# A two-layer encoder with eight experts: 20 weight slots of 1 MB in place of 17, and two branches a scatter in place of four

## The chip, the cores and the metric

The kernel runs on one core of a Trainium2 chip. Time is device time in microseconds from the start to the end of one execution. The core has five engines with a queue of instructions each: PE (matrix products into PSUM), DVE (vector), ACT (scalar functions), POOL and SP. SP issues the weight DMAs. Engines wait for each other by semaphores.

## The reference

Two layers over 272 tokens (16 meta tokens and 256 of input) of width 1024. Each layer has four mixers and a feed-forward part; that of the second layer is a mixture of eight experts, of which each token takes two:

```python
logits = (t @ router).astype(jnp.float32)
top_v, top_i = lax.top_k(logits, TOP_K)
gates = jax.nn.softmax(top_v, axis=-1)
combine = jnp.sum(jax.nn.one_hot(top_i, N_EXPERTS) * gates[..., None], axis=1)
out = jnp.zeros_like(t)
for e in range(N_EXPERTS):
    out = out + combine[:, e:e + 1] * _swiglu(t, wg[e], wu[e], wd[e])
```

with `_swiglu(u, wg, wu, wd) = (silu(u @ wg) * (u @ wu)) @ wd`. An expert is 3584 wide, all in float32, and the eight of them have 352 MB of weights. After the second layer comes a last RMSNorm.

## The kernel before

**Up to the experts.** Layer 1, then the mixers of layer 2 and its output projection. While that projection runs, `stat_logit` (L1262) turns the residual back to rows of tokens (`hr`) and takes the sums of squares (L1281, with a scratch tile `jk` that nobody reads). Then the router picks two experts for each token and counts the tokens of each expert.

**An expert.** Its tokens are gathered by a product with a 0/1 matrix (`pick`, tile `xe`, up to 96 tokens). The 3584 columns go in 7 steps of 512. A step has four weight tiles of 1 MB for the gate and up products (`gate_up`, tiles `gu` and `gx`) and two for the down product (`down`, tile `dn`, summed in PSUM over the steps). 8 experts of 7 steps of 6 tiles are 336 DMAs. Each product has a first part for 64 tokens and a second part for the other 32 that is executed only if the expert has more than `CA` = 64 tokens: `more` (L1380) puts it under `tc.If(n > CA)`, a conditional branch on PE. In the text an expert with more is heavy, one with fewer is light.

**The order on PE** is the program's own order (a manual schedule, L1547): in step i the first half of `gate_up`, then `between`, then the second half, then the down product of step i-1. `between` turns the activations of step i-1 (`turn_sg`, PSUM tile `ehT`, copied out by ACT at L1468 into `eh`). In the third step of an expert it also scatters the expert before.

**The scatter** (L1506) adds the gated result `oe`, and `oe4` for tokens 65 to 96, to the tokens' rows. The result has two halves `i` of 512 columns and two halves `j` of 128 tokens, so four products into four PSUM tiles `sct`. Each has a first matmul (L117), two conditional ones (a pair, L116), and an addition to `acc` on DVE (L1517). `ehT`, `sct` and the tiles of `turn` and `pick` share two PSUM banks in turn: `pp = lambda n='pp': bank('pp', n, 2)`. The scatter of expert 7 follows at the end of the program, and after it the last norm (`final`), which reads the weight row `fin` and writes squares to `jk`.

**The weight tiles.** `eload` gives each tile the next slot in a fixed rotation that a string names by pool: b (4 slots), c (6), a (3), o (2), and u and U, two tiles of the dense part that have become free; 17 in all. One further slot (h) serves once, and becomes `acc`. SP issues the DMAs in the order of use and waits before each until its slot has been read. `ahead` issues the first 18 as soon as their memory is free, during the output projection.

Of the kernel before, what the change touches and what calls it, by code (L numbers as in the profile page):

```python
# [9 lines left out]
F32 = mybir.dt.float32  # L10
# [4 lines left out]
ALU = mybir.AluOpType  # L15
# [6 lines left out]
D = 1024  # L22
DC = 8
# [4 lines left out]
C = 96  # L28
# [80 lines left out]
def build(tc, A, out, off):  # L109
    nc = tc.nc  # L110
    ctx = ExitStack()
    V, SC, GP, PE = nc.vector, nc.scalar, nc.gpsimd, nc.tensor

    def mm(o, a, b, start=True, stop=True, skip=False):
        if skip:
            return PE.matmul(o, a, b, start=start, stop=stop, skip_group_check=True)  # L116
        return PE.matmul(o, a, b, start=start, stop=stop)  # L117
# [3 lines left out]
    def bank(tag, name, bufs):  # L121
        return ps.tile([128, 512], F32, tag=tag, name=name, bufs=bufs)

    pp = lambda n='pp': bank('pp', n, 2)
# [113 lines left out]
    bs = mb_('stat')  # L238
# [18 lines left out]
    for a0, w in ((0, 272), (272, 271)):  # L257
        b = mb_('fb')
# [908 lines left out]
    with tc.tile_pool(name='fw', bufs=1, reuse_waits='tile') as fw, \  # L1167
# [22 lines left out]
        def fload(*a):  # L1190
            fcnt[0] += 1
            return wload({'a': wa, 'b': wb}['aaabb'[(fcnt[0] - 1) % 5]], *a)
# [3 lines left out]
        def fsplit(w):  # L1196
            scnt[0] += 1
            k, f = w.shape[1], w.shape[2]
            if scnt[0] % 3 != 2:
                hl = [fw.tile([128, 2048], F32R, tag='fw', name='fw', bufs=4)[:, :k * f].rearrange('p (k f) -> p k f', k=k)  # L1200
                      for _ in range(2)]
                split(*hl, w)
                return [[t[:, i] for i in range(k)] for t in hl]
            k = k // 2
            hl = [], []
            for i in range(2):
                t = wo.tile([128, 2048], F32R, tag='w', name='wx')
                t = [t[:, 1024 * p_:1024 * p_ + k * f].rearrange('p (k f) -> p k f', k=k) for p_ in range(2)]
                split(*t, w[:, k * i:k * i + k])
                for p_ in range(2):  # L1210
                    hl[p_].extend(t[p_][:, kk] for kk in range(k))
            return hl
# [25 lines left out]
        for m2 in range(4):  # L1238
            b = [(mb_, bm, pp)[m2 % 3]('dn') for _ in range(2)]
            for k0, nk in ((0, 8), (8, 8), (16, 6)):  # L1240
                w = fsplit(fload(A['ffn_w_down'][0, 128 * k0:128 * (k0 + nk), 256 * m2:256 * m2 + 256], nk, 256))
# [4 lines left out]
            for mi in range(2):  # L1246
                m = 2 * m2 + mi
                t = fp.tile([128, L], F32, name='sg', tag='sg', bufs=2)
# [14 lines left out]
    def stat_logit(h, m):  # L1263

        if not lgp:
            lgp.append(bm('lg'))
        with tc.manual_schedule(engines={mybir.EngineType.PE}):
            for j in range(2):
                t0 = TOK[j][0]
                mm(lgp[0][:, NE * j:NE * j + NE], h[:, t0:t0 + 128], rt[:, m, :], start=(m == 0 and j == 0),  # L1270
                   stop=(m == DC - 1), skip=True)
        n, c = m // 4, m % 4
        if c == 0:
            hrb.extend(bm('hr') for _ in range(2))
        for j in range(2):
            t0 = TOK[j][0]
            PE.transpose(hrb[j][:, 128 * c:128 * c + 128], h[:, t0:t0 + 128], ident)
        if c == 3:
            for j in range(2):
                jk = ep.tile([128, 512], F32, name='jk', tag='jk', bufs=2)  # L1280
                SC.activation(jk, hrb[j], AF.Square, accum_out=sj[:, 2 * j + n:2 * j + n + 1])  # L1281
            for j in range(2):
                SC.copy(hr[:, j, 512 * n:512 * n + 512], hrb[j])
            del hrb[:]
# [3 lines left out]
    wb = ctx.enter_context(tc.tile_pool(name='wb2', bufs=4, side='right', reuse_waits='tile'))  # L1288
    mq = ctx.enter_context(tc.tile_pool(name='mq', bufs=1, reuse_waits='tile'))
    ep = ctx.enter_context(tc.tile_pool(name='ep', bufs=1, reuse_waits='tile'))  # L1290
# [4 lines left out]
    def rstd_rows(r, ss):  # L1295
        V.tensor_scalar(r, ss, 1.0 / D, EPS, op0=ALU.mult, op1=ALU.add)
        GP.tensor_tensor(r, r, nhalf[:, :2], op=ALU.pow)
# [38 lines left out]


    cnt, wdma = [0], []
    wc = ctx.enter_context(tc.tile_pool(name='wc', bufs=6, reuse_waits='tile'))
    slots = {'a': wa, 'b': wb, 'c': wc, 'o': wo}  # L1340
    wm = A['moe_w']
    nb = FE // 512
# [21 lines left out]
    def dn_units(w, fb):  # L1364
        return [(w[fb, u], 2) for u in (4, 5)]

    first, order = 'bbbbccccccaaaoouUh', 'bbbbccccccaaaoouU'

    def ahead(slots_, i):

# [10 lines left out]
    def more(n, body):  # L1381

        if n is None:
            return body()
        with tc.If(n > CA):  # L1385
            body()
# [41 lines left out]
    def new_xe():  # L1428
        return ep.tile([128, DC, C], F32, name='xe', tag='xe', bufs=2)
# [32 lines left out]
    def turn_sg(sg, s4):  # L1462
        b = pp('ehT')
        for i in range(2):
            PE.transpose(b[:, 128 * i:128 * i + 128], sg[:, 128 * i:128 * i + 128], ident)  # L1465
        PE.transpose(b[:, 256:384], s4, ident)  # L1466
        eh = ep.tile([128, 384], F32, name='eh', tag='eh', bufs=2)
        SC.copy(eh, b[:, :384])  # L1468
        return eh
# [35 lines left out]

    def scatter(oe, oe4, GT, GT4, n, to, fro):  # L1506
        for i in range(2):
            for j in range(2):
                b = pp('sct')
                mm(b, GT[:, 128 * j:128 * j + 128], oe[:, i])  # L1510

                def rest():
                    for p_ in range(2):
                        mm(b, GT4[:, 128 * j:128 * j + 128], oe4[p_][:, i], start=False, stop=(p_ == 1), skip=True)

                more(n, rest)
                V.tensor_tensor(to[:, j, 512 * i:512 * i + 512], fro[:, j, 512 * i:512 * i + 512], b, op=ALU.add)  # L1517

    sel_of = lambda e: select([rk[:, j, e:e + 1] for j in range(2)], [gat[:, j, e:e + 1] for j in range(2)], rx)
    banks = lambda: [bm('dn') for _ in range(3)]  # L1520
# [49 lines left out]
                sgs[i] = act(*bgu)  # L1570


    def final(fin, res):
        for n in range(2):
            fs = slice(512 * n, 512 * n + 512)
            for j in range(2):
                h = acc[:, j, fs]
                jk = ep.tile([128, 512], F32, name='jk', tag='jk', bufs=2)
                SC.activation(jk, h, AF.Square, accum_out=sj[:, 2 * j + n:2 * j + n + 1])  # L1579
                (GP if j in [1] else V).tensor_tensor(res[:, j, fs], h, fin[:, fs], op=ALU.mult)  # L1580
        V.tensor_tensor(rj, sj[:, 0::2], sj[:, 1::2], op=ALU.add)  # L1581
        rstd_rows(rj, rj)
        for j in range(2):
            for n in range(2):
                fs = slice(512 * n, 512 * n + 512)
                if (j, n) == (0, 1):
                    SC.activation(res[:, j, fs], res[:, j, fs], AF.Copy, scale=rj[:, j:j + 1])
                else:
                    V.tensor_scalar(res[:, j, fs], res[:, j, fs], rj[:, j:j + 1], None, op0=ALU.mult)  # L1589
            nc.sync.dma_start(out[0, 128 * j:128 * j + 128, :], res[:, j])  # L1590

    with tc.high_priority(200):
        eh = turn_sg(*sgs.pop(i))
    fin = ep.tile([128, D], F32, name='fin', tag='fin')
    finish(i, eh)
    with tc.issue_after(wdma[-1].ins):
        SP.dma_start(fin, A['final_norm_w'][None, :].to_broadcast([128, D]))
    scatter(*gated(dn[NE - 1], T_[NE - 1][2]), *T_[NE - 1][:2], nr[NE - 1], acc, acc)
    res = up.tile([128, DC * L], F32, name='res', tag='uTl')[:, :2 * D].rearrange('p (j f) -> p j f', j=2)
    final(fin, res)  # L1600


    most = nc.values_load(mxi[0:1, 0:1], min_val=0, max_val=S)  # L1603
    with tc.If(most > C):
        rk2 = ep.tile([128, 2, NE], F32, name='rk2')
        V.tensor_copy(rk2, rk)
        order = 'abab'
        for _ in range((S - 1) // C):
            V.tensor_scalar(rk2, rk2, -float(C), None, op0=ALU.add)
            with tc.For_i(0, NE, 1) as e:  # L1610
                rc = ep.tile([128, 2, 2], F32, name='rc')
                V.tensor_copy(rc[:, 0, :], rk2[:, :, bass.ds(e, 1)].rearrange('p j o -> p (j o)'))
                V.tensor_copy(rc[:, 1, :], gat[:, :, bass.ds(e, 1)].rearrange('p j o -> p (j o)'))
                w = wm[bass.ds(e, 1)].rearrange('o b u p f -> (o b) u p f')
                sl = select([rc[:, 0, j:j + 1] for j in range(2)], [rc[:, 1, j:j + 1] for j in range(2)], rx)
                GT, GT4, gc = turn(*sl)
                xe = new_xe()
                for k4 in range(2):
                    pick(xe, sl[2], k4)
                do = banks()  # L1620
                for fb in range(nb):
                    down(do, turn_sg(*act(*gate_up(xe, w, fb, None))), w, fb, None)
                scatter(*gated(do, gc), GT, GT4, None, acc, acc)
        fin = ep.tile([128, D], F32, name='fin', tag='fin')
        GP.dma_start(fin, A['final_norm_w'][None, :].to_broadcast([128, D]))
        final(fin, res)
    ctx.close()


# [43 lines left out]
```

## Time and profile before

| | |
|---|---|
| median of 3 runs | 1489.84 us (1486.25 to 1493.8) |
| the profiled execution | 1490.97 us |
| its span, first to last instruction | 1489.1 us |
| PE busy | 1424.5 us, 96% |
| DVE, ACT, POOL busy | 537.5, 356.0, 81.0 us |
| granted clock of PE, mean | 0.978 |
| moved by DMA | 429.22 MB, mean 288 GB/s |

A row of the table of stretches has, in this order, the busy time of PE, of PE's weight loads, of DVE, ACT and POOL. Two views are read below by their idle time: a row of the timeline has the start, the time taken and, in brackets, how long the engine had been idle and who ended that. A row of the waits adds such idle time up by who ended it. A busy engine isn't necessarily one at its full speed, and a wait for several semaphores is put down to the one that came last.

### The profile page before, as it was taken

The page shows a single profiled execution, that of the slowest core. Times are in us where ns is not written, and L with a number is a line of the kernel's source. Part 1 is how long each engine was busy: PE and PEld are TensorE (multiplying, and loading weights), DVE is VectorE, ACT ScalarE, POOL GpSimd, SP SyncE. Part 2 cuts the span into 40 slices and gives each one's busy share as a digit, 9 for nine tenths or more (in the row PEclk, how much of TensorE's full clock was granted, in tenths as well). Part 3 has the DMA queues.
Part 4 walks back from the last instruction along what each step waited for, and adds up shares of the span by engine and source line. Part 5 has one row for each costly group of instructions (what it writes and reads, how often), then busy time and mean ns, then how long its engine had stood idle before and what let it go on. Part 6 is the DMA issues. An engine that isn't in the chain of part 4 may idle for free. (4 is left out here: it accounts for less than half of the span.)

```text
span 1489.1 us, 30433 instructions
## 1 busy us (share of the span) xinstructions
PE 1424.5 (96%) x13288; PEld 1011.9 (68%) x13288; DVE 537.5 (36%) x1179; ACT 356.0 (24%) x716; POOL 81.0 (5%) x77
## 2 busy tenths in 40 slices
PE   7999989999989999999999999999999999999996
PEld 6887789999988869656555565455555455555552
DVE  6885476555667775200211200211200211202102
ACT  4544344444453543000100100100100101101002
POOL 4141000000012300000000000000000000000000
PEclk9999699999999999999999999999999999999998
DMA  9521075555433309888999999999999999999980
GB/s 278 164 86 57 1 218 171 180 167 165 126 100 116 112 31 414 317 341 339 384 418 417 418 419 376 390 418 419 418 412 373 405 418 419 417 417 420 419 338 31
DMA packets 116442, 429.22 MB, mean 288 GB/s; under 512 B 7900, under 2 KB 69852, under 8 KB 73008
## 3 DMA queue, kind: packets, MB, share of 16 engines
q1 hardware_dynamic: 116032, 425.48, 73.6%
q8 instruction: 140, 2.29, 0.6%
q0 software_dynamic: 240, 1.19, 0.2%
q14 instruction: 30, 0.25, 0.0%
HBM read 425.59 MB, written 2.17 MB: 287 GB/s over the span
## 5 line engine op out<-in xcount | busy, mean ns | idle before, releaser
L116 PE MATMUL gu<-w,xe 128*64 128x256 f32 x3584 | 411.7, 382 | 12.6 <-PEq L1385 7.9
L116 PEld LDWEIGHTS gu<-w,xe 128*64 128x64 f32 x3584 | 261.3, 137 | 168.4 <-issue 64.5
L116 PE MATMUL dn<-w,eh 128*64 128x512 f32 (+1 forms) x1344 | 257.1, 598 | 8.1 <-PEq L1385 7.7
L116 PEld LDWEIGHTS dn<-w,eh 128*64 128x64 f32 (+1 forms) x1344 | 77.1, 127 | 156.3 <-issue 155.2
L1459 DVE TENSOR_TENSOR es<-es,gx 128x128 f32<-128x128 f32 x56 | 16.1, 287 | 422.5 <-ACT es L1458 422.5
L1468 ACT COPY eh<-ehT 128x384 f32<-128x384 f32 x56 | 26.8, 478 | 466.1 <-PE ehT L1466 457.8
L116 PE MATMUL gx<-w,xe 128*32 128x128 f32 x3584 | 109.4, 274 | 0.0
L116 PEld LDWEIGHTS gx<-w,xe 128*32 128x32 f32 x3584 | 94.4, 110 | 21.5 <-issue 21.5
L142 ACT CAST wx<-w 128x1024 fp32r<-128x1024 f32 (+2 forms) x86 | 87.9, 1026 | 68.2 <-PE wo L1132 16.7
L143 DVE TENSOR_TENSOR wx<-w,wx 128x1024 fp32r<-128x1024 f32 (+2 forms) x75 | 89.7, 1202 | 33.7 <-ACT wx L142 33.4
L1458 ACT ACTIVATE es<-gx 128x128 f32<-128x128 f32 x56 | 15.5, 277 | 288.4 <-PE gx L116 171.0
L1132 PE MATMUL wo<-mixh,wx 128*128 128x272 f32 (+1 forms) x256 | 58.8, 311 | 6.0 <-DVE hT L1135 4.9
L1424 DVE TENSOR_TENSOR xe<-xe,fwc 128x384 f32<-128x384 f32 x16 | 8.9, 558 | 144.6 <-PE xe L117 144.6
L143 DVE TENSOR_TENSOR fw<-w,fw 128x2048 fp32r<-128x2048 f32 (+1 forms) x23 | 50.6, 2199 | 26.4 <-ACT fw L142 26.4
L1132 PEld LDWEIGHTS wo<-mixh,wx 128*128 128x128 f32 x256 | 44.2, 197 | 12.8 <-DVE hT L1135 6.3
L142 ACT CAST fw<-w 128x2048 fp32r<-128x2048 f32 (+1 forms) x23 | 42.1, 1832 | 37.0 <-PE dn L160 16.2
L1580 POOL TENSOR_TENSOR res<-acc,fin 128x512 f32<-128x512 f32 x2 | 2.9, 1458 | 881.4 <-DVE acc L1517 881.4
L1517 DVE TENSOR_TENSOR acc<-acc,sct 128x512 f32<-128x512 f32 x28 | 18.9, 687 | 51.5 <-PEq L1385 35.1
L161 PE MATMUL g<-uTh,fw 128*128 128x272 f32 x128 | 37.0, 289 | 0.0
L160 PE MATMUL g<-uTl,fw 128*128 128x272 f32 x128 | 36.8, 288 | 0.0
L159 PE MATMUL g<-uTh,fw 128*128 128x272 f32 x128 | 36.5, 288 | 0.0
L1134 PE MATMUL wo<-mixl,wx 128*128 128x272 f32 (+1 forms) x128 | 35.0, 295 | 0.0
(488 smaller groups left out, 2311.4 us busy)
## 6 DMA issues: line engine op xcount, KB each, us to landing
w<-in_moe_w SPq DMA_DIRECT2D x336, 1024.0 KB, 14.7
w<-in_w_in SPq DMA_DIRECT2D x20, 1024.0 KB, 5.3
w<-in_ffn_w_gate SPq DMA_DIRECT2D x11, 1024.0 KB, 5.5
w<-in_ffn_w_up SPq DMA_DIRECT2D x11, 1024.0 KB, 5.4
w<-in_w_out SPq DMA_DIRECT2D x8, 1024.0 KB, 5.0
w<-in_ffn_w_down SPq DMA_DIRECT2D x8, 1024.0 KB, 5.3
w<-in_ffn_w_down SPq DMA_DIRECT2D x4, 768.0 KB, 4.5
w<-in_w_in SPq DMA_DIRECT2D x4, 512.0 KB, 5.7
```

Of the source, the lines that this page charges most:

```text
L116: return PE.matmul(o, a, b, start=start, stop=stop, skip_group_check=True)
L142: a = SC.copy(hi, src)
L143: return a, (eng or V).tensor_tensor(lo, src, hi.bitcast(F32), op=ALU.subtract)
L159: PE.matmul(o, a[0], b[0], start=start, stop=False)
L160: PE.matmul(o, a[0], b[1], start=False, stop=False)
L161: PE.matmul(o, a[1], b[0], start=False, stop=stop)
L1132: PE.matmul(o, a, mixT[0][:, c0 + k, q0:], start=(p_ == k == 0), stop=(p_ == k == 1))
L1134: PE.matmul(o, a, mixT[1][:, c0 + k, q0:], start=False, stop=False)
L1458: SC.activation(t, b_[:, :w], AF.Silu)
L1459: V.tensor_tensor(t, t, b_[:, w:2 * w], op=ALU.mult)
L1468: SC.copy(eh, b[:, :384])
L1517: V.tensor_tensor(to[:, j, 512 * i:512 * i + 512], fro[:, j, 512 * i:512 * i + 512], b, op=ALU.add)
```

## The change

Pool `wc` gets 9 slots in place of 6, and the rotation 20 in place of 17. Room for them is made in three places: the scratch `jk` of the sums of squares lies in the slots of `xe`, the final norm's row and its scratch in a weight slot of pool b (`last_tiles`), and the memory for POOL's DMA descriptors is set to 8192 bytes. The scatter takes both `j` of a half together: two first matmuls, one branch over both pairs, two additions.

```diff
@@ stat_logit
-                jk = ep.tile([128, 512], F32, name='jk', tag='jk', bufs=2)
+                jk = ep.tile([128, DC, C], F32, name='jk', tag='xe', bufs=2).rearrange('p k c -> p (k c)')[:, :512]
@@
-    wc = ctx.enter_context(tc.tile_pool(name='wc', bufs=6, reuse_waits='tile'))
+    wc = ctx.enter_context(tc.tile_pool(name='wc', bufs=9, reuse_waits='tile'))
@@
-    first, order = 'bbbbccccccaaaoouUh', 'bbbbccccccaaaoouU'
+    first, order = 'bbbbcccccccccaaaoouUh', 'bbbbcccccccccaaaoouU'
@@ scatter
         for i in range(2):
+            bs = [pp('sct') for _ in range(2)]
             for j in range(2):
-                b = pp('sct')
-                mm(b, GT[:, 128 * j:128 * j + 128], oe[:, i])
-
-                def rest():
+                mm(bs[j], GT[:, 128 * j:128 * j + 128], oe[:, i])
+
+            def rest():
+                for j in range(2):
                     for p_ in range(2):
-                        mm(b, GT4[:, 128 * j:128 * j + 128], oe4[p_][:, i], start=False, stop=(p_ == 1), skip=True)
-
-                more(n, rest)
-                V.tensor_tensor(to[:, j, 512 * i:512 * i + 512], fro[:, j, 512 * i:512 * i + 512], b, op=ALU.add)
+                        mm(bs[j], GT4[:, 128 * j:128 * j + 128], oe4[p_][:, i], start=False, stop=(p_ == 1), skip=True)
+
+            more(n, rest)
+            for j in range(2):
+                V.tensor_tensor(to[:, j, 512 * i:512 * i + 512], fro[:, j, 512 * i:512 * i + 512], bs[j], op=ALU.add)
@@
+    def last_tiles():
+        t = wb.tile([128, 2048], F32, name='fin', tag='w')
+        return t[:, :D], [t[:, D + 512 * j:D + 512 * j + 512] for j in range(2)]
...
-    fin = ep.tile([128, D], F32, name='fin', tag='fin')
     finish(i, eh)
     with tc.issue_after(wdma[-1].ins):
+        fin, jks = last_tiles()
         SP.dma_start(fin, A['final_norm_w'][None, :].to_broadcast([128, D]))
...
-    nc = bacc.Bacc("TRN2", target_bir_lowering=False, num_devices=1)
+    nc = bacc.Bacc("TRN2", target_bir_lowering=False, num_devices=1, dynamic_dma_scratch_size=8192)
```

The order on PE, in the first scatter (expert 0, in the third step of expert 1), from its first matmul. The number in `sct_7801` is that of the PSUM tile, and in brackets stands whose semaphore the instruction waits for. Before:

```order
L117 MATMUL sct_7801<-oe_7576,GT_6499 128x512
L1385 COMPARE_AND_BRANCH
L116 MATMUL sct_7801<-oe4_7577,GT_6499 128x512 x2
L1385 UNCONDITIONAL_BRANCH
L1385 UNCONDITIONAL_BRANCH [waits PE_49]
L117 MATMUL sct_7807<-oe_7576,GT_6499 128x512 [waits Activation_49]
L1385 COMPARE_AND_BRANCH
L116 MATMUL sct_7807<-oe4_7577,GT_6499 128x512 x2
L1385 UNCONDITIONAL_BRANCH
L1385 UNCONDITIONAL_BRANCH [waits PE_49]
L117 MATMUL sct_7813<-oe_7576,GT_6499 128x512 [waits DVE_49]
L1385 COMPARE_AND_BRANCH
```

And in the changed kernel:

```order
L117 MATMUL sct_7801<-oe_7576,GT_6505 128x512
L117 MATMUL sct_7802<-oe_7576,GT_6505 128x512 [waits Activation_49]
L1385 COMPARE_AND_BRANCH
L116 MATMUL sct_7801<-oe4_7577,GT_6505 128x512 x2
L116 MATMUL sct_7802<-oe4_7577,GT_6505 128x512 x2
L1385 UNCONDITIONAL_BRANCH
L1385 UNCONDITIONAL_BRANCH [waits PE_49]
L117 MATMUL sct_7812<-oe_7576,GT_6505 128x512 [waits DVE_49]
L117 MATMUL sct_7813<-oe_7576,GT_6505 128x512 [waits DVE_49]
L1385 COMPARE_AND_BRANCH
```

The second first matmul has moved ahead of the branch and of the first pair, with its wait for ACT. Both first matmuls of the second half wait for DVE, as before, but now one behind the other with no branch between them.

The order on DVE in the same scatter (`hr` is the residual, `acc` the sum). Before:

```order
L1517 TENSOR_TENSOR acc_6378<-hr_5939,sct_7801 128x512 [waits DMAHW6_49,PE_49]
L1385 UNCONDITIONAL_BRANCH x2
L1517 TENSOR_TENSOR acc_6378<-hr_5939,sct_7807 128x512 [waits PE_49]
L1517 TENSOR_TENSOR acc_6378<-hr_5939,sct_7813 128x512 [waits PE_49]
L1385 UNCONDITIONAL_BRANCH
L1517 TENSOR_TENSOR acc_6378<-hr_5939,sct_7819 128x512 [waits PE_49]
```

And in the changed kernel:

```order
L1519 TENSOR_TENSOR acc_6384<-hr_5939,sct_7801 128x512 [waits DMAHW1_49,PE_49]
L1519 TENSOR_TENSOR acc_6384<-hr_5939,sct_7802 128x512 [waits PE_49]
L1385 UNCONDITIONAL_BRANCH
L1519 TENSOR_TENSOR acc_6384<-hr_5939,sct_7812 128x512 [waits PE_49]
L1519 TENSOR_TENSOR acc_6384<-hr_5939,sct_7813 128x512 [waits PE_49]
```

The additions stand in pairs between the ends of the branches, each with its own wait for PE.

The order on SP, from the last DMA of the output projection's weights. Before:

```order
L138 DMA w<-in_w_out 128x2x1024 x4
L1352 DMA w<-in_moe_w 128x2048 x18
L1603 TENSOR_LOAD mxi
L1603 ISA x2
L1385 UNCONDITIONAL_BRANCH
L1352 DMA w<-in_moe_w 128x2048 x2
L1385 UNCONDITIONAL_BRANCH
```

And in the changed kernel:

```order
L138 DMA w<-in_w_out 128x2x1024 x4
L1352 DMA w<-in_moe_w 128x2048 x21
L1609 TENSOR_LOAD mxi
L1609 ISA x2
L1385 UNCONDITIONAL_BRANCH
L1352 DMA w<-in_moe_w 128x2048 x2
L1385 UNCONDITIONAL_BRANCH
```

Three more weight DMAs stand ahead of the first one that is tied to the experts' own progress.

## Rows read from the trace of the kernel before

**Rows 1.** Stretches: us, busy time (instructions) by engine, granted clock, DMA share, GB/s.

```profile
602.00:735.00 133.00, 131.81 (x1708) 77.46 (x1708) 17.00 (x48) 9.10 (x26) 0.00 (x0) 1.00 0.88 337
735.00:835.00 100.00, 94.56 (x802) 56.33 (x802) 19.66 (x45) 11.01 (x28) 0.00 (x0) 1.00 1.01 418
```

**Rows 2.** Waits of PE, 600 to 1471 us: total us, times, longest us.

```profile
PE gu L116 <- DMA w<-in_moe_w: 3.3, 4, 1.0
```

**Rows 3.** Timeline of PE near 1345 us: start us, us, instruction, [idle before].

```profile
1344.91 1.30 PE L116 MATMUL gu<-w,xe 128*64 128x256 f32 x10 [0.99 <-PEq L1385]
```

**Rows 4.** Line 1352, 1319.5 to 1320.5 us: one weight DMA.

```profile
L1352 SPq DMA_DIRECT2D w<-in_moe_w x1: 328/328/328, 1319.8 to 1319.8; - x1
...
DMA to landing us min/median/max: 19.9/19.9/19.9
```

**Rows 5.** Line 1352, 557 to 594 us: the first 18 weight DMAs.

```profile
L1352 SPq DMA_DIRECT2D w<-in_moe_w x18: 327/365/448, 557.1 to 593.1; - x18
...
DMA to landing us min/median/max: 4.7/9.9/15.8
```

**Rows 6.** Timeline: a down product of expert 7, issue and first reader of fin.

```profile
1425.60 5.51 PE L116 MATMUL dn<-w,eh 128*64 128x512 f32 x32
...
1430.86 0.33 SPq L1597 DMA_DIRECT2D fin<-in_final_norm_w  x1
...
1475.13 1.27 POOL L1580 TENSOR_TENSOR res<-acc,fin 128x512 f32<-128x512 f32 x1 [879.48 <-DVE acc L1517]
```

**Rows 7.** DMA issues of the whole run: KB each, median us from issue to landing.

```profile
fin<-in_final_norm_w SPq DMA_DIRECT2D x1, 512.0 KB, 20.1
```

**Rows 8.** Timeline: the scatter of expert 0, a heavy one.

```profile
750.50 0.48 PE L117 MATMUL sct<-oe,GT 128*128 128x512 f32 x1
...
750.84 0.48 ACT L1468 COPY eh<-ehT 128x384 f32<-128x384 f32 x1 [8.01 <-PE ehT L1466]
...
751.37 0.50 PE L117 MATMUL sct<-oe,GT 128*128 128x512 f32 x1
...
751.71 0.63 PE L116 MATMUL sct<-oe,GT 128*128 128x512 f32 x2
...
752.38 0.69 DVE L1517 TENSOR_TENSOR acc<-hr,sct 128x512 f32<-128x512 f32 x1 [0.20 <-PE sct L116]
...
753.45 0.62 PE L116 MATMUL sct<-oe,GT 128*128 128x512 f32 x2
...
754.00 2.37 PE L116 MATMUL gu<-w,xe 128*64 128x256 f32 x19
```

**Rows 9.** Timeline: the scatter of expert 1, a light one.

```profile
853.61 0.47 PE L117 MATMUL sct<-oe,GT 128*128 128x512 f32 x1
...
854.48 1.12 PE L117 MATMUL sct<-oe,GT 128*128 128x512 f32 x2 [0.39 <-ACT eh L1468]
...
855.11 2.06 DVE L1517 TENSOR_TENSOR acc<-acc,sct 128x512 f32<-128x512 f32 x3 [0.21 <-PEq L1385]
...
855.85 0.50 PE L117 MATMUL sct<-oe,GT 128*128 128x512 f32 x1 [0.25 <-DVE acc L1517]
...
856.50 2.34 PE L116 MATMUL gu<-w,xe 128*64 128x256 f32 x19
```

**Rows 10.** Instructions on the tile sct, whole run: count, ns min/median/max, first and last.

```profile
L116 PE MATMUL sct<-oe,GT x32: 387/392/398, 750.8 to 1477.2; 128*128 128x512 f32 x32
```

**Rows 11.** Timeline: the scatter of expert 7, at the end.

```profile
1472.67 0.50 PE L117 MATMUL sct<-oe,GT 128*128 128x512 f32 x1 [1.56 <-DVE oe L1500]
...
1473.67 1.38 DVE L1517 TENSOR_TENSOR acc<-acc,sct 128x512 f32<-128x512 f32 x2 [1.05 <-PE sct L116]
...
1475.08 0.76 DVE L1500 SCALAR_TENSOR_TENSOR oe<-dn,gc,oe 64x512 fp32r<-64x512 f32 x1
...
1475.90 0.50 PE L117 MATMUL sct<-oe,GT 128*128 128x512 f32 x1 [1.57 <-DVE oe L1500]
...
1476.99 1.29 DVE L1517 TENSOR_TENSOR acc<-acc,sct 128x512 f32<-128x512 f32 x2
```

More of the change, by code (lines that the diff above doesn't have):

```diff
@@ L1570, in build, with final @@
                 sgs[i] = act(*bgu)
-    def final(fin, res):
+    def last_tiles():
+        t = wb.tile([128, 2048], F32, name='fin', tag='w')
+        return t[:, :D], [t[:, D + 512 * j:D + 512 * j + 512] for j in range(2)]
+    def final(fin, jks, res):
         for n in range(2):
@@ L1577, in final @@
                 h = acc[:, j, fs]
-                jk = ep.tile([128, 512], F32, name='jk', tag='jk', bufs=2)
+                jk = jks[j]
                 SC.activation(jk, h, AF.Square, accum_out=sj[:, 2 * j + n:2 * j + n + 1])
@@ L1599, in build @@
     res = up.tile([128, DC * L], F32, name='res', tag='uTl')[:, :2 * D].rearrange('p (j f) -> p j f', j=2)
-    final(fin, res)
+    final(fin, jks, res)
     most = nc.values_load(mxi[0:1, 0:1], min_val=0, max_val=S)
@@ L1623, in build @@
                 scatter(*gated(do, gc), GT, GT4, None, acc, acc)
-        fin = ep.tile([128, D], F32, name='fin', tag='fin')
+        fin, jks = last_tiles()
         GP.dma_start(fin, A['final_norm_w'][None, :].to_broadcast([128, D]))
-        final(fin, res)
+        final(fin, jks, res)
     ctx.close()
```

## The prediction

> **What bounds the kernel now.** I read the table of stretches first, to see which stage the change lies in. The experts run from 602 to 1471 us of the 1489.1 us span, and TensorE (PE) is busy in nearly all of it: 131.81 of 133 us in the stretch 602 to 735, where the expert has over 64 tokens ("heavy", the conditional part of each product is executed), and 94.56 of 100 us in 735 to 835, where it is skipped ("light") [rows 1]. In the light stretches the DMA engines are full as well (share 1.01, 418 GB/s), so two things could set the pace. A full DMA with a PE that is 95% busy is what a weight-bound loop can look like, so busy shares don't decide it. The second view does: PE's waits between 600 and 1471 us. The wait put down to a weight DMA is 3.3 us in 4 places, at most 1.0 us each [rows 2]. The last of the four places is at 1344.91 us, the first gate product of expert 7, 0.99 us idle, which another view puts down to PE's own sequencer [rows 3]. The weights which that product reads were issued at 1319.8 us and landed 19.9 us later [rows 4], that is at 1339.7, 5.2 us before use. So the four waits are the start of an expert, where the sequencer reads the token count, and no lack of weights. I followed all 336 weight DMAs from landing to first use in the same way, and the stretch around 1340 us is the tightest. **PE alone sets the pace from 602 to 1471 us, and every time added to or taken from PE there goes into the end time in full.**
>
> **The slots.** Three more slots (wc from 6 to 9) let the queue run 3 MB further ahead. At 418 GB/s a slot of 1.05 MB takes 2.5 us, so the lead grows by 3 x 2.5 = 7.5 us wherever the queue had been stopped by full slots. PE takes the same weights at the same time as before, so I cost this at 0. At the start nothing comes late either: the first 18 DMAs are issued by 593.1 us and land within 15.8 us [rows 5], so by 608.9; the three added ones stand behind them and land by about 616, when PE is in its first steps with the tiles that came first.
>
> The places found for the slots cost nothing by the same kind of cover. The scratch of the row sums now lies in the two xe slots: the last write of it precedes the first xe of expert 0 on the way to it. The final norm's row (fin) goes into a weight slot. It was issued at 1430.86 us and is first read at 1475.13; the slot that it takes was last read by a down product that ended at 1431.1 us (1425.60 + 5.51), some 6 us later in the new kernel, and with the 20.1 us that it took to land it is there by 1458 [rows 6, 7]. If that cover failed, it would be POOL and VectorE (DVE) at the end that wait. Halving the descriptor space touches only the four DMAs that POOL issues in the setup of the program.
>
> **The scatter, heavy.** A scatter has two halves; each has two first matmuls, two conditional pairs, two adds on DVE, and two PSUM banks in all. Before, bank 1's pair covered the wait for bank 2, and bank 2's matmuls covered the add of bank 1. Now both banks are taken at once, and the next half can't begin before the first add has ended. Before [rows 8]: first matmul 750.50, second 751.37 (it waits for ACT's copy out of the bank, 750.84 + 0.48), next gate product 754.00: 3.50 us. Now, from the first matmul as 0: the second at 0.87, since it takes the same bank. The pairs follow 0.34 after it (751.37 to 751.71), 0.46 apart (a pair takes 0.63 and a matmul 0.39 [rows 10], so there are about 0.23 between two starts): 1.21 and 1.67; the first is done at 1.84. Its add starts 0.04 later (751.71 + 0.63 to 752.38), 1.88, and takes 0.69: 2.57. The next half's first matmul comes 0.05 after (as 855.11 + 0.69 to 855.85 [rows 9]): 2.62. The second add follows the first by 0.60 to 0.69 (two adds take 1.29 and 1.38 [rows 11]); with 0.62 it ends at 3.19, second matmul 3.24, pairs 3.58 and 4.04, and the gate product 0.55 after the last pair's start (753.45 to 754.00): 4.59. That is **+1.09 us**.
>
> **The scatter, light.** Before [rows 9]: 853.61 to 856.50, 2.89 us. Now: second matmul again at 0.87 (854.48), the skip and the first add 0.63 after it (854.48 to 855.11), so 1.50; add ends 2.19, second add at 2.12 ends at 2.81, the second matmul of the second half 2.86, and the gate product 0.65 after (855.85 to 856.50): 3.51. That is **+0.62 us**.
>
> [...]
>
> **How often.** 32 conditional matmuls [rows 10] at 8 a heavy scatter are 4 heavy scatters of 8. One of them is expert 7's at the end, so 3 heavy and 4 light ones lie in the loop: 3 x 1.09 + 4 x 0.62 = 5.75 us.
>
> **The end.** Expert 7's scatter [rows 11] starts at 1472.67, both banks free. Now the second matmul is 0.23 behind, pairs at 1473.24 and 1473.70, first add at 1473.91 instead of 1473.67. DVE makes the second half's operand behind the two adds, so 1475.08 becomes 1475.32. In the second half the first add starts 1.24 after its first matmul (0.23 + 0.34 + 0.63 + 0.04), at 1476.14 + 1.24 = 1477.38 instead of 1476.99; the second add ends at 1478.7 instead of 1478.28 (1476.99 + 1.29), and the square of it on ACT follows. That is **+0.4 us**, on the path to the output.
>
> **Sum.** 0 + 5.75 + 0.4 = +6.15 us on the profiled execution, which took 1490.97 us: 1497.1. It lies 1.13 us above the median of the runs (1489.84), so against that I forecast **1496.0 us**.
>
> Bounds of the new waits. If no add ever held PE, a light scatter's second half would begin 0.65 after the matmul at 0.87 (the two from 854.48 take 1.12 together), so 1.52, 1.75, and the gate product at 2.40 (-0.49); a heavy one's 0.32 behind the last matmul of the pairs (0.55 less 0.23), so 2.22, 2.45, pairs 2.79 and 3.25, gate product 3.80 (+0.30): 4 x -0.49 + 3 x 0.30 = -1.1 us. If both adds began only behind the branch and both had to end before the next half, light is 1.50 + 2 x 0.69 = 2.88, matmuls 2.93 and 3.16, gate product 3.81 (+0.92); heavy 2.34 + 1.38 = 3.72, matmuls 3.77 and 4.00, pairs 4.34 and 4.80, gate product 5.35 (+1.85); the end loses 0.46 more in each half, +1.4 in all: 3.7 + 5.5 + 1.4 = +10.6 us. I take the value between, since the waits before 854.48 and 855.85 [rows 9] show PE held by exactly these two releases, ACT's copy and one add of DVE.
>
> **Rivals.** (A) The weights bound the loop after all, and PE's busy time hides it. For it: 418 GB/s for 100 us on end [rows 1]. Against it: the 5.2 us of lead at the tightest place. Then the scatters' delays fall into waits and the 7.5 us of lead come off: 1490.97 - 7.5 + 0.4 = 1483.9, against the median 1482.8. Faster. (B) The removed branches pay and the waits don't come: two conditional steps fewer in each of 8 scatters. For it: a pair stands 0.34 behind its first matmul, 0.11 more than the 0.23 between two matmuls. Against it: in the old scatter that time lies beside the adds. The sum is the lower bound: 1490.97 - 1.1, against the median 1488.7.
>
> [...]
>
> (C) The bank wait is dearer: the first add starts only behind both pairs, and PE stands through both adds, in the heavy and the light scatters alike. For it: after the branch DVE has both adds in one block. Against it: the first add needs only its own bank. It decides if a heavy scatter takes over 5 us; the time is the upper bound, +10.6: 1501.6, against the median 1500.5. Slower.
>
> **How the numbers follow.** About 0.5% (7.4 us) is what a measurement of this kernel can tell from no change, so "the same" is 1482.4 to 1497.3. Forecast 0.70, A 0.08, B 0.12, C 0.10. The forecast's own range is 1492 to 1500, since each of its latencies is read from one or two rows and the median of three runs moves by 2 us; about 0.28 of it lies over 1497.3. Slower: 0.70 x 0.28 + 0.10 = 0.30. Faster: half of A and a little noise, 0.05. Same: 0.65. The range reaches from B (1488) to a little over C (1501.5); A's end is left out.
>
> **What would show it.** Right: in the new profile a heavy scatter lasts about 4.6 us from its first matmul to the next gate product and a light one 3.5; PE's wait for DVE's adds and ACT's copy at the scatter grows; gate, up and down blocks keep their lengths; the lead of the weights at its tightest place grows from about 5 to over 10 us, with no change of the end; the last add ends about 0.4 us later behind PE's last down product. Wrong: PE blocks that get shorter or start earlier where the lead had been small (A), scatters of 2.4 us (B) or over 5 us (C), or a stretch before 602 us that has moved.

## The result, and the profile after

| | before | changed |
|---|---|---|
| median | 1487.88 us (14 runs, 1482.77 to 1497.53) | 1495.6 us (14 runs, 1490.22 to 1510.56) |
| ratio to before, 95% interval | | 1.0058 (1.0032 to 1.0083) |
| the profiled execution, its span | 1490.97 us, 1489.1 | 1510.56 us, 1508.8 |
| first gate product of the experts | 602.82 us | 612.59 us |
| from there to the end of the last down product | 868.30 us | 878.60 us |

The changed kernel is slower by 0.3 to 0.8%, that is 5 to 12 us; 6.15 us were forecast. The profiled execution is the slowest of its 14, so its 19.7 us more of span must be divided first. 9.8 us are there before the first gate product. The stretch 120 to 200 us shows where from; first the kernel before, then the changed one, then a second profile of the changed one (below as e8). The columns are those of [rows 1]; the third number from the right is the granted clock.

```profile
120.00:200.00 80.00, 77.37 (x455) 57.80 (x453) 43.91 (x136) 28.54 (x74) 4.31 (x6) 0.81 0.17 53
```

```profile
120.00:200.00 80.00, 79.71 (x389) 58.14 (x389) 37.79 (x124) 25.66 (x71) 4.35 (x6) 0.65 0.07 21
```

```profile
120.00:200.00 80.00, 76.91 (x466) 56.60 (x466) 46.12 (x139) 30.25 (x77) 4.30 (x6) 0.84 0.20 60
```

In the changed kernel's first profile TensorE ran at a mean of 0.65 here and got through 389 matmuls in place of 455. The second profile of the same kernel has 0.84, and its first gate product is at 601.57 us. So this delay belongs to one execution, not to the change, and the experts' stage is what can be compared: 868.30 us before, 878.60 us after, **10.3 us more**.

Within that stage the two views that answer to [rows 1] and [rows 2]: the table of stretches, and PE's waits from 610 to 1491 us (total us, times, longest).

```profile
612.00:745.00 133.00, 131.81 (x1709) 77.41 (x1710) 17.16 (x49) 9.32 (x26) 0.00 (x0) 1.00 0.93 364
745.00:845.00 100.00, 93.74 (x783) 55.76 (x779) 18.74 (x44) 10.78 (x27) 0.00 (x0) 1.00 1.01 418
```

```profile
PE sct L117 <- DVE acc L1519: 4.5, 7, 0.9
PE sct L117 <- ACT eh L1468: 3.0, 7, 0.7
PE gu L116 <- DMA w<-in_moe_w: 1.6, 3, 1.0
```

PE is as busy as before in the heavy stretch (131.81 us) and a little less in the light one. The waits for weights have not become more. At the scatter PE now waits seven times for an add and seven times for ACT's copy, once for each scatter in the loop, 7.5 us in all. Before, from 600 to 1471 us, it was 2.8 us:

```profile
PE sct L117 <- ACT eh L1468: 1.8, 5, 0.4
...
PE sct L117 <- DVE acc L1517: 1.0, 4, 0.3
```

The scatter of expert 0, heavy, answers to [rows 8] (timeline of the changed kernel):

```profile
760.28 0.47 PE L117 MATMUL sct<-oe,GT 128*128 128x512 f32 x1
...
761.15 0.50 PE L117 MATMUL sct<-oe,GT 128*128 128x512 f32 x1 [0.39 <-ACT eh L1468]
...
761.49 1.07 PE L116 MATMUL sct<-oe,GT 128*128 128x512 f32 x4
762.14 1.28 DVE L1519 TENSOR_TENSOR acc<-hr,sct 128x512 f32<-128x512 f32 x2 [7.68 <-PE sct L116]
...
762.88 1.10 PE L117 MATMUL sct<-oe,GT 128*128 128x512 f32 x2 [0.32 <-DVE acc L1519]
...
764.83 0.44 PE L116 MATMUL gu<-w,xe 128*64 128x256 f32 x2
```

From the first matmul: second at 0.87, pairs at 1.21, first add at 1.86, second half at 2.60, gate product at 4.55. The forecast had 0.87, 1.21, 1.88, 2.62 and 4.59. The scatter of expert 1, light, answers to [rows 9]:

```profile
864.23 0.48 PE L117 MATMUL sct<-oe,GT 128*128 128x512 f32 x1
...
865.10 0.49 PE L117 MATMUL sct<-oe,GT 128*128 128x512 f32 x1 [0.39 <-ACT eh L1468]
865.72 1.28 DVE L1519 TENSOR_TENSOR acc<-acc,sct 128x512 f32<-128x512 f32 x2 [10.18 <-PEq L1385]
...
866.46 1.10 PE L117 MATMUL sct<-oe,GT 128*128 128x512 f32 x2 [0.87 <-DVE acc L1519]
...
867.71 5.36 PE L116 MATMUL gu<-w,xe 128*64 128x256 f32 x32
```

3.48 us, where 3.51 were forecast. But the last row holds what was not: the 32 gate products behind the light scatter take 5.36 us. Before, they took 3.67 behind every scatter. The table of stretches shows why (the granted clock is again third from the right). First the light scatter of expert 1 and its gate block in the kernel before:

```profile
853.61:856.50 2.89, 1.95 (x7) 0.75 (x6) 2.02 (x4) 0.48 (x1) 0.00 (x0) 1.00 1.03 420
856.50:860.18 3.68, 3.68 (x36) 2.69 (x40) 0.67 (x1) 0.00 (x0) 0.00 (x0) 1.00 1.00 416
```

Then the same place in the changed kernel, and the last light scatter of its loop:

```profile
855.00:864.23 9.23, 9.23 (x124) 4.91 (x120) 0.54 (x2) 0.00 (x0) 0.00 (x0) 1.00 1.02 421
864.23:867.71 3.48, 1.98 (x7) 0.75 (x6) 1.30 (x3) 0.48 (x1) 0.00 (x0) 1.00 1.01 414
867.71:871.30 3.59, 3.59 (x19) 2.51 (x21) 1.27 (x2) 0.00 (x0) 0.00 (x0) 0.54 1.03 429
871.30:873.07 1.77, 1.77 (x20) 1.17 (x20) 0.00 (x0) 0.00 (x0) 0.00 (x0) 0.96 1.01 421
...
1402.72:1406.21 3.49, 1.97 (x7) 0.75 (x6) 1.30 (x3) 0.48 (x1) 0.00 (x0) 1.00 1.01 420
1406.21:1410.06 3.85, 3.85 (x36) 2.32 (x40) 1.26 (x2) 0.00 (x0) 0.00 (x0) 1.00 1.03 423
```

In the light scatter PE is busy for 1.98 of 3.48 us, where it was 1.95 of 2.89 before; right behind it, at the third place already in its last part (from 1301.5 us, 0.3 us ahead of the gate block), the clock falls to 0.50 for some 3.4 us (here from 868.0 to 871.4 us) and comes back to 1.00. The DMA goes on as before (share 1.03, 429 GB/s), so nothing lacks weights. This happens behind three of the four light scatters (gate blocks of 5.36, 5.36 and 5.17 us, 4.9 us more than 3 x 3.67), and not behind the last one.

The lead of the weights answers to [rows 3, 4]. The tightest weight now is one of expert 7; its DMA, and the gate block whose second half reads it:

```profile
DMA to landing us min/median/max: 21.4/21.4/21.4
```

```profile
1380.04 3.67 PE L116 MATMUL gu<-w,xe 128*64 128x256 f32 x32 [0.31 <-PEq L1385]
```

Issued at 1347.2, landed at 1368.5, first read at 1381.8: a lead of 13.3 us where the tightest was 4.5 before (the second weight of the product in [rows 3]; the prediction named the first, with 5.2). The end answers to [rows 11]:

```profile
1492.74 0.73 PE L117 MATMUL sct<-oe,GT 128*128 128x512 f32 x2 [1.56 <-DVE oe L1500]
...
1497.33 1.29 DVE L1519 TENSOR_TENSOR acc<-acc,sct 128x512 f32<-128x512 f32 x2 [0.17 <-PE sct L116]
```

The last adds start 4.59 us behind the scatter's first matmul, 4.32 before: 0.27 us later. The way from the last down product to the last instruction doesn't show it: it took 17.99 us before, and 17.60 and 18.39 us in the two profiles of the changed kernel.

### The profile page after: what moved, and what is told of

It reads as the page before. It is cut to its first block, busy times and chain, and to the rows that moved or that the text cites. A ratio compares the mean times of both kernels' runs of the same rounds, so it can differ in the third digit from the quotient of the medians.

```text
span 1508.8 us, 30396 instructions
## 1 busy us (share of the span) xinstructions
PE 1439.8 (95%) x13288; PEld 1021.5 (68%) x13288; DVE 537.3 (36%) x1179; ACT 356.2 (24%) x716; POOL 80.9 (5%) x77
## 5 line engine op out<-in xcount | busy, mean ns | idle before, releaser
L116 PE MATMUL gu<-w,xe 128*64 128x256 f32 x3584 | 416.6, 385 | 12.7 <-PEq L1385 9.8
L1468 ACT COPY eh<-ehT 128x384 f32<-128x384 f32 x56 | 26.8, 478 | 466.0 <-PE ehT L1466 457.7
L160 PE MATMUL g<-uTl,fw 128*128 128x272 f32 x128 | 36.8, 288 | 0.0
```

Source lines behind the costliest of these rows:

```text
L160: PE.matmul(o, a[0], b[1], start=False, stop=False)
```

## The experiments

The theory after this comparison: the slots are worth nothing here, the scatter costs by its waits for two shared PSUM banks, and the idle time in the light scatters costs a second time, by the clock. The table holds all runs. "Stage" is the time from the first gate product to the end of the last down product in the profile; "lead" is the smallest time between a weight's landing and its first use, over all 336.

| kernel | median us (runs) | ratio to before (95%) | stage us | light, heavy scatter us | lead us |
|---|---|---|---|---|---|
| before | 1487.88 (14); beside e1 to e4 1487.77 (29), beside e5 to e8 1487.93 (31) | | 868.30 | 2.89, 3.50 | 4.5 |
| changed | 1495.6 (14) | 1.0058 (1.0032 to 1.0083) | 878.60 | 3.48, 4.55 | 13.3 |
| e1: 20 slots, scatter of before | 1486.65 (12) | 0.9989 (0.9964 to 1.0014) | 868.19 | 2.88, 3.51 | 13.1 |
| e2: 17 slots, new scatter | 1502.19 (6) | 1.0101 (1.0067 to 1.0134) | 878.73 | 3.49, 4.55 | 7.5 |
| e3: changed, a third bank | 1483.73 (12) | 0.9981 (0.9961 to 1.0000) | 865.08 | 2.23, 3.32 | 9.2 |
| e4: changed, idle time filled | 1494.65 (10) | 1.0042 (1.0023 to 1.0062) | 874.19 | 3.49, 4.56 | 14.6 |
| e5: before, 14 slots | 1493.31 (10) | 1.0035 (1.0013 to 1.0058) | 871.61 | 2.88, 3.49 | 0.0 |
| e6: 20 slots, halves in two steps | 1483.14 (12) | 0.9975 (0.9945 to 1.0005) | 862.64 | 1.72, 3.16 | 9.1 |
| e7: 17 slots, halves in two steps | 1481.42 (12) | 0.9948 (0.9922 to 0.9975) | 861.58 | 1.72, 3.12 | 2.6 |
| e8: changed, again | 1496.59 (8) | 1.0058 (1.0037 to 1.0079) | 878.97 | 3.48, 4.55 | 15.7 |
| e9: before, one bank | 1514.66 (1; before 1498.18) | | 894.39 | 5.04, 6.58 | 12.6 |

The lengths are those of the first scatter of each kind. The part ahead of the experts differs between executions (first gate product at 612.59 us with a granted clock of 0.65 between 120 and 200 us, at 601.57 us with 0.84), so the stage tells more than the median where they differ; but it is that of one execution.

Each run also has its mean granted clock on record. An estimate of what a run lost to the clock is its span times one less that clock, and the rest is its time at full clock, as in the gate block at 867.71 us, where some 3.4 us at 0.50 made 5.36 us of 3.67 (medians, us; the third digit of the clock makes 1.5 us in one run):

| | before | changed, e8 | e1 | e2 | e3 | e4 |
|---|---|---|---|---|---|---|
| at full clock | 1457.4, 1456.6 | 1463.2, 1462.9 | 1456.6 | 1463.5 | 1452.7 | 1463.1 |
| lost to the clock | 26.8, 28.2 | 31.4, 31.4 | 28.2 | 36.8 | 31.1 | 29.9 |

The two values of the kernel before are those of its runs beside e1 to e4 and beside e5 to e8. At full clock the changed kernel, e2 and e4 agree, 5.5 to 6.9 us over the kernel before and e1. The time lost to the clock varies with the part ahead of the experts as well: e3 lost 31.1 us, and its stage has no fall of the clock.

**e1, the slots alone.** The changed kernel with `scatter` as it was.

```diff
+            for j in range(2):
+                b = pp('sct')
+                mm(b, GT[:, 128 * j:128 * j + 128], oe[:, i])
...
+                more(n, rest)
```

> The changed kernel with the scatter of before (four branches). Theory (the slots cost and give nothing, all of the loss is the scatter's): ratio to before 1.000, within 0.3%; the expert stage, from the first gate product to the last down product, as long as before to 0.5 us; heavy scatter 3.5 us, light 2.9, the gate block behind each 3.67; lead of the weights at the tightest place over 10 us in place of 5. Rival A (the weights bound the loop): the expert stage 7.5 us shorter, ratio 0.995. A third possibility, that the slots or the places found for them cost something themselves: expert stage longer by more than 1 us, ratio over 1.002.

Stage 868.19 against 868.30 us, ratio 0.9989 with 1 inside the interval, and a lead of 13.1 us: the lead grew by 8.6 us and bought nothing. Rival A is refuted, and so is a cost of the places found for the slots.

**e2, the scatter alone.** The kernel before with the new `scatter`, 17 slots.

> The kernel before with the two-branch scatter alone. Theory: heavy scatter 4.55 us, light 3.49, so 3 x 1.06 + 4 x 0.6 = 5.6 us more, and on top the half clock in the gate blocks behind light scatters (up to 1.7 us each, 0 to 6.8 us in all, 5.1 in the profile of the changed kernel): expert stage 5.6 to 12.4 us longer, ratio 1.004 to 1.008. The lead of the weights at its tightest place is no smaller than 5 us, since PE is later. Rival (the loss needs the new slots too): ratio below 1.002, and the gate blocks behind light scatters 3.67 us.

The stretches of its first light scatter and of the gate block behind it:

```profile
849.76:853.25 3.49, 1.98 (x7) 0.76 (x6) 1.30 (x3) 0.48 (x1) 0.00 (x0) 0.98 1.01 415
853.25:856.80 3.55, 3.55 (x18) 2.35 (x20) 1.27 (x2) 0.00 (x0) 0.00 (x0) 0.54 1.01 420
```

The scatter, the fall of the clock and the stage (878.73 us) are those of the changed kernel. The whole loss of the stage is the scatter's. The median of its six runs lies higher than the stage explains (1.0101). By the estimate above the clock accounts for it: these runs lost 36.8 us to it, 5.4 more than the changed kernel's, and at full clock they take the same time (1463.5 against 1463.2 us). That six runs had so low a clock isn't explained.

**e3, a third bank.** In the changed kernel the second tile of the first half goes to the pool of `gu` and `gx`, of whose three banks one is free at that place.

```diff
-            bs = [pp('sct') for _ in range(2)]
+            bs = [pp('sct'), (mb_ if i == 0 else pp)('sct')]
```

> The changed kernel, but the second tile of the scatter's first half lies in the third bank of the pool of gu and gx, which is free there, so that the first half has both banks at once and the second half has to wait for one add only. Theory (the price is the wait for the two shared banks, the branches saved are worth something by themselves): light scatter about 2.25 us in place of 3.48 (before 2.89), heavy about 3.3 in place of 4.55 (before 3.50), the gate block behind a light one 3.67 with a granted clock of 1.0; the expert stage 3 us shorter than before (4 x 0.64 + 3 x 0.17), ratio to before 0.998. Rival (merging the branches itself is what costs, through later adds or the branch's own length): light and heavy stay over 2.9 and 3.5, ratio over 1.001.

The light scatter of expert 1 in the timeline, and the stretches of it and of its gate block:

```profile
852.71 0.71 PE L117 MATMUL sct<-oe,GT 128*128 128x512 f32 x2
...
853.57 0.50 PE L117 MATMUL sct<-oe,GT 128*128 128x512 f32 x1 [0.15 <-ACT eh L1468]
...
854.29 0.49 PE L117 MATMUL sct<-oe,GT 128*128 128x512 f32 x1 [0.21 <-DVE acc L1519]
```

```profile
852.71:854.94 2.23, 1.71 (x8) 0.68 (x6) 1.31 (x3) 0.48 (x1) 0.00 (x0) 1.00 1.01 415
854.94:858.61 3.67, 3.67 (x36) 2.68 (x40) 1.53 (x3) 0.00 (x0) 0.00 (x0) 1.00 1.01 417
```

Two merged branches stand here as in the changed kernel, yet the scatter is shorter than before (2.23 and 3.32 us), the waits have shrunk to 0.15 and 0.21 us, and the clock holds. The stage is 3.2 us shorter than before, 3 were expected. The wait for the bank, not the merged branch, is what cost.

**e4, work in the idle time.** Three matmuls ahead of each second half.

```diff
+            if i == 1:
+                fill = mb_('fill')
+                for _ in range(3):
+                    mm(fill, GT[:, 0:128], oe[:, 0])
```

> The changed kernel with three extra matmuls (128x512, into a spare PSUM bank that nobody reads) ahead of the second half of each scatter, where PE waits for the add: PE works in that time. Theory (the clock falls because PE stands idle for a good part of the light scatter): the light scatter is 3.5 to 3.8 us long, and the gate block behind it 3.67 us at a granted clock of 1.0; the heavy scatter grows to 4.7 to 5.2 us, since it has less idle time to fill. Rival (the clock falls for another reason, as the branch, DVE's adds beside the gate block or a fixed rhythm): at least two of the four gate blocks behind light scatters still take over 5 us, at a granted clock near 0.5.

The stretches of its first light scatter and of the gate block behind it:

```profile
848.69:852.18 3.49, 2.70 (x10) 1.24 (x9) 1.57 (x4) 0.48 (x1) 0.00 (x0) 1.00 1.00 411
852.18:855.85 3.67, 3.67 (x36) 2.68 (x40) 1.27 (x2) 0.00 (x0) 0.00 (x0) 1.00 1.02 426
```

The same 3.49 us, but PE busy for 2.70 of them in place of 1.98, and all four gate blocks behind light scatters are 3.67 us at full clock. The stage is 5.9 us longer than before, which is the scatters' 5.6 us and hardly more: without the fall of the clock the forecast's own sum appears. In the medians the gain isn't clear of noise: 1.0042 and 1.0058 have intervals that overlap, and the runs of e4 lost 1.5 us less to the clock than those of the changed kernel, where the profiles differ by 4.4 us of stage. One expectation missed: the heavy scatter didn't grow (4.56 us), since the three matmuls fit into its waits too.

**e5, fewer slots.** Pool c with 3 slots, 14 in all, in the kernel before.

```diff
-    wc = ctx.enter_context(tc.tile_pool(name='wc', bufs=6, reuse_waits='tile'))
+    wc = ctx.enter_context(tc.tile_pool(name='wc', bufs=3, reuse_waits='tile'))
...
-    first, order = 'bbbbccccccaaaoouUh', 'bbbbccccccaaaoouU'
+    first, order = 'bbbbcccaaaoouUh', 'bbbbcccaaaoouU'
```

> The kernel before with three slots fewer (pool c with 3, 14 slots in all) and its four-branch scatter. Theory (a slot is worth 2.5 us of lead and costs nothing as long as the lead stays over zero): the tightest lead of before, 4.5 us in expert 6, becomes 4.5 - 7.5 = -3.0, so PE waits about 3 us in all for weights near 1340 us and nowhere else (the next tightest experts have 17 us); the expert stage is 2 to 4 us longer, ratio to before 1.001 to 1.003; all scatters as before. Rival A (the weights bound the loop all the time): at least 7.5 us longer, with waits in many experts. Rival (slots don't set the lead): no wait, the same length.

PE near 1340 us (timeline, without its weight loads):

```profile
1339.25 1.95 PE L116 MATMUL gu<-w,xe 128*64 128x256 f32 x16 [0.65 <-DMA w<-in_moe_w]
1341.64 1.95 PE L116 MATMUL gu<-w,xe 128*64 128x256 f32 x16 [0.44 <-DMA w<-in_moe_w]
...
1349.19 1.94 PE L116 MATMUL dn<-w,eh 128*64 128x512 f32 x8 [0.64 <-DMA w<-in_moe_w]
```

Here is what a wait for weights looks like: one tile after another, at the pace of the DMA (416 to 422 GB/s here, by which 1.05 MB take 2.5 us), each first used 0.04 to 0.14 us after it has landed. The stage is 3.3 us longer; the lead of 4.5 less 3 x 2.5 us has PE lack 3.0. So slots are worth something below 17 and nothing above, for a PE as fast as this one.

**e6 and e7, the halves in two steps.** The first half of the scatter stays in the third step of an expert, the second moves to the fourth; each has one bank of the shared pool and one of the pool of `gu`. e6 has 20 slots, e7 has 17.

```diff
-    def scatter(oe, oe4, GT, GT4, n, to, fro):
-        for i in range(2):
-            bs = [pp('sct') for _ in range(2)]
+    def scatter(oe, oe4, GT, GT4, n, to, fro, halves=range(2)):
+        for i in halves:
+            bs = [pp('sct'), mb_('sct')]
...
-                if fb == 2 and e > 0:
-                    scatter(*oes.pop(e - 1), *T_.pop(e - 1)[:2], nr[e - 1], acc, hr if e == 1 else acc)
+                if fb in (2, 3) and e > 0:
+                    scatter(*oes[e - 1], *T_[e - 1][:2], nr[e - 1], acc, hr if e == 1 else acc, [fb - 2])
```

> The changed kernel with the two halves of the scatter in two successive steps of the expert (the third and the fourth), each with one tile from the shared pool and one from the pool of gu and gx. Theory (the price is the wait for banks; where none is waited for, the saved branches pay): each half 0.88 us when light and 1.58 when heavy, so 1.76 and 3.16 for a scatter in place of 3.48 and 4.55 (before 2.89 and 3.50), no gate block over 3.9 us, the expert stage 4 x 1.13 + 3 x 0.34 = 5.5 us shorter than before (868.3), ratio to before about 0.996. Rival (the two branches of a scatter cost by themselves, or the halves meet other waits in the fourth step): halves over 1.1 and 1.8 us, stage no shorter than 865 us, ratio over 0.998.

> The same halves in two steps, with 17 slots. Theory: PE is 4.4 us earlier at the tightest place of the weights (3 heavy and 3 light scatters lie ahead of it), so the lead of 4.5 us falls to about 0; PE waits for weights not at all or by less than 1 us, the expert stage 5 to 5.5 us shorter than before. Rival (slots are worth more than the lead shows): the stage is more than 2 us longer than with 20 slots.

A heavy half and a light half in the timeline of e7:

```profile
749.31 0.71 PE L117 MATMUL sct<-oe,GT 128*128 128x512 f32 x2
...
749.86 1.10 PE L116 MATMUL sct<-oe,GT 128*128 128x512 f32 x4
750.53 1.28 DVE L1519 TENSOR_TENSOR acc<-hr,sct 128x512 f32<-128x512 f32 x2 [7.30 <-PE sct L116]
...
750.88 0.65 PE L116 MATMUL gu<-w,xe 128*64 128x256 f32 x4
```

```profile
851.92 0.71 PE L117 MATMUL sct<-oe,GT 128*128 128x512 f32 x2
...
852.75 1.28 DVE L1519 TENSOR_TENSOR acc<-acc,sct 128x512 f32<-128x512 f32 x2 [9.80 <-PEq L1385]
852.77 1.08 PE L116 MATMUL gu<-w,xe 128*64 128x256 f32 x8
```

No row of PE in the loop waits for an add any more: the adds run beside the gate block. The stage is 5.7 us (e6) and 6.7 us (e7) shorter than before, with 5.5 expected. e7 is faster than the kernel before (0.9948, 0.9922 to 0.9975), and so than the changed one; e6's interval takes in 1 (0.9945 to 1.0005). It has 17 slots: its lead of 2.6 us (about 0 was expected) is just enough, and three more slots again bring nothing. That e6 is 1.1 us longer is one pause of PE of 1.27 us ahead of a down product at 723.63 us, whose weights had landed by 680; its cause the profile doesn't show.

**e8, the changed kernel again.**

> The changed kernel again, for a second profile. Theory: scatters 4.55 and 3.48 us again, expert stage 5.8 us longer than before and on top the half clock behind light scatters; how much of it comes is open (0 to 6.8 us, by where the clock's rhythm meets the scatters; 5.1 in the first profile). The 9.84 us by which the experts began later in the first profile belong to that execution (granted clock 0.68 and 0.63 between 120 and 200 us): the first gate product is back near 602 us. Rival (the places found for the slots delay the part ahead of the experts): the first gate product is again after 608 us.

Its gate blocks behind the first three light scatters:

```profile
857.17:860.70 3.53, 3.53 (x18) 2.28 (x20) 1.27 (x2) 0.00 (x0) 0.00 (x0) 0.53 1.03 427
...
1078.83:1082.40 3.57, 3.57 (x18) 2.55 (x20) 1.27 (x2) 0.00 (x0) 0.00 (x0) 0.52 1.01 420
...
1291.50:1295.00 3.50, 3.50 (x22) 2.37 (x24) 1.26 (x2) 0.00 (x0) 0.00 (x0) 0.65 1.01 419
```

The clock falls at the same three places (0.53, 0.52 and 0.65), as it does in the profile of e2 (0.54 at the first), and the stage is 878.97 us (878.60 in the first profile), while the experts begin at 601.57. So the fall is there in all three profiles with the new scatter on two shared banks, and the late start isn't. Of the rhythm in the expectation this much is shown: in the first profile the clock is at 0.50 for 3.41 us at each of the three places, from 868.02, 1089.88 and 1301.51 us, and from start to start it is 65 and 62 times 3.413 us.

**e9, the waits without the merged branch.** In the kernel before one tile serves all four products of a scatter.

```diff
     def scatter(oe, oe4, GT, GT4, n, to, fro):
+        b = pp('sct')
         for i in range(2):
             for j in range(2):
-                b = pp('sct')
```

> The kernel before with all four products of a scatter in one and the same PSUM tile: still four branches and single adds, but each product waits for the add before it. Theory (PE's idle time in the scatter is what lets the clock fall, not the merged branch): light scatter 3 x 1.37 + 0.65 = 4.8 us, PE busy for under half of it, heavy about 6.1; the gate blocks behind light scatters over 4.5 us in at least two of four places at a granted clock near 0.5, or the fall comes already within the scatter. Rival (the merged branch or the paired adds are needed for it): scatters as long, but every gate block 3.67 us and the clock 1.0.

A heavy scatter with its gate block, and the last light one with its own (stretches):

```profile
1195.73:1202.35 6.62, 4.28 (x17) 2.11 (x15) 2.06 (x3) 0.48 (x1) 0.00 (x0) 0.91 1.01 413
1202.35:1207.09 4.74, 4.73 (x33) 2.65 (x32) 0.69 (x1) 0.00 (x0) 0.00 (x0) 0.77 0.98 401
...
1400.49:1405.22 4.73, 1.97 (x7) 0.75 (x6) 2.08 (x4) 0.48 (x1) 0.00 (x0) 1.00 1.02 419
1405.22:1410.58 5.36, 5.36 (x36) 3.75 (x40) 0.67 (x1) 0.00 (x0) 0.00 (x0) 0.68 1.02 423
```

With four branches and single adds, the clock falls in or behind all four light scatters (0.59 to 0.77 in the gate blocks) and two of the three heavy ones (0.75 and 0.77; 1.00 behind the other). This is one execution, but together with e4 (no fall with PE busy for 2.70 of 3.49 us, a fall here with 1.97 of 4.73) it leaves PE's idle time as the cause, and not the form of the branch or the adds. Which part of the idle time counts stays open: the longest pause in a light scatter is 0.87 us in the changed kernel and 0.39 us in e4, and its sum goes from 1.50 to 0.79 us at the same time.

## Why the prediction was right, and what it lacked

**What bounds the kernel.** Right. e1 makes the lead 8.6 us larger and the stage stays; e5 takes the lead away and PE waits at the place that the prediction named, near 1340 us. One row was misread on the way: of the four waits put down to a weight DMA, three are the 1.0 us at 815.08, 1033.35 and 1251.89 us and one has 0.3 us; the 0.99 us at 1344.91 us is not among them. The conclusion stands: all four pauses of 1.0 us are the first gate product of an expert, and in the changed kernel the view puts the first three down to the sequencer and the one of expert 7 to the DMA, with the same 0.99 to 1.06 us.

**The slots at 0.** Right, by e1 to 0.1 us of stage. The cover for `fin` held too: issued at 1451.24 us, with 9.6 us to landing, it is there some 34 us before its first reader.

**The scatters.** Right, step by step: heavy +1.05, +1.04 and +1.08 us for +1.09 each, light +0.59, +0.59, +0.61 and +0.61 for +0.62; together 5.57 us for 5.75. The two releases that were chosen between the bounds, one add and ACT's copy, are those that the waits of the changed kernel name.

**The end.** +0.27 us on the way to the last adds, for +0.4; the end of the program varies by more than that. (The upper bound counted +1.4 there, where 0.4 and twice 0.46 make 1.3.)

**What it lacked.** "Gate, up and down blocks keep their lengths" was wrong. The sum had no term for the clock: 4.9 us in the first profile, 4.5 in the second (5.29, 5.36 and 4.88 us, less 3 x 3.67). With it the sum would have been 6.15 + 4.9 = 11 us; the two profiles have 10.3 and 10.7 us in the stage, the medians 7.7 and 8.7, with an interval of 5 to 12. By the estimate from the runs' clocks, the changed kernel takes 5.5 to 6.6 us more at full clock, which is the forecast's own sum, and loses 3.2 to 4.6 us more to the clock; whether the clock falls at these places in every run isn't shown. That the forecast's 1496.0 us lies so close to 1495.6 was luck: the kernel before ran at a median 2.0 us lower than in the three runs that the forecast started from, and the loss came out 1.6 us larger than forecast. A hint was there: of the light scatter before, PE is busy for 1.95 of 2.89 us, at a full clock, and the prediction added 0.62 us that are idle nearly in full.

**The rivals.** A is refuted by e1. B, that saved branches pay, may have a true half: with the bank waits cut the merged scatter is shorter than the old one by 0.2 to 0.7 us (e3) and by 0.4 to 1.2 us (e7). But in the light scatter 0.64 us of that can be the old scatter's own waits ([rows 9]: 0.39 and 0.25 us), and four branches with a third bank were not run, so what two branches fewer save by themselves isn't shown. In the changed kernel the waits cost more than the merge can have saved. C needed a heavy scatter of over 5 us; they took 4.55 to 4.85.

## What to carry to other kernels

Before buffers are added, measure the smallest lead of the stream over its use: where it was over zero, as the 4.5 us here, three more slots bought nothing (e1: a stage of 868.19 us against 868.30), and the room is better spent elsewhere. Before two steps are merged to save a branch, count the PSUM banks that the merged step holds at once and who frees each; a bank that is idle in another pool, or half the work moved to another step, made the same merged scatter shorter than the old one (light: 2.23 us in e3 and 1.72 in e7, against 2.89). And price an added wait on TensorE twice: its own length, and the lower clock that can follow it (here 0.6 us in a light scatter, and 1.5 to 1.7 us in the gate block behind three of the four).

## What the runs showed of the hardware that was not expected

- The granted clock fell to 0.50 for 3.41 us right behind a stretch in which PE was busy for 1.98 of 3.48 us, and did not fall behind 1.95 of 2.89 (before), 2.70 of 3.49 (e4) or 1.71 of 2.23 (e3). Pauses between matmuls went ahead of it: PE's longest in the light scatter was 0.87 us.
- The fall isn't sure: behind the last light scatter the clock stayed at 1.00 in the first profile, with the same 1.97 of 3.49 us. Two profiles of the changed kernel and that of e2 agree on the three places where it fell, and what picks them was not tried; in e9 it fell at the last place too.
- Three matmuls nobody needs, in the waits, cost nothing (scatters of 3.49 and 4.56 us as without them) and gave 4.4 us of stage back in the profiles (874.19 against 878.60); the medians of the runs differ by too little to show it.
- The part ahead of the experts, with instructions that the change leaves in order, differed by 11 us between two executions (first gate product 612.59 and 601.57 us), at granted clocks of 0.65 and 0.84 between 120 and 200 us.
